# Ten issue edges on VectorE and ScalarE in a decoder step that TensorE fills

## The chip, the cores and the metric

The kernel runs on one core of a Trainium2 chip. Its engines are TensorE (PE in the profile; PEld is its weight load), VectorE (DVE), ScalarE (ACT), GpSimd (POOL), and SyncE (SP), whose queue issues nearly all DMAs. Each engine takes the instructions of its own queue in the order in which the program lists them; an instruction that waits for another engine holds up what stands behind it. The metric is the time of one execution on the device in microseconds (us), as the median of several runs. A profiled execution gives the trace; times of the trace count from the start of its span.

## The reference

The kernel computes one layer of a hybrid decoder for a prompt of 2048 tokens and for 8 sequences of one further token each, all in fp32, with a model width of 1024:

```
xn = rmsnorm(x, norm1_g);  z = xn @ w_in                 # 1024 -> 512 | 512 | 512 | 128 | 128
xr, gr, q, k, v = split(z)
xc = causal_conv4(xr);  r, i = sigmoid(block_diag(xc))   # real-gated LRU, a scan over the tokens
rec = lru(xc, r, i) * gelu(gr)
att = windowed_attention(q, k, v, sinks)                 # self + 128 previous tokens, 8 heads, 2 kv heads
mix = concat(rmsnorm(rec), rmsnorm(att));  h = x + mix @ w_out
hn = rmsnorm(h, norm2_g)
y = h + (silu(hn @ w_gate) * (hn @ w_up)) @ w_down       # d_ff 2816
return rmsnorm(y, final_norm_g), new k, v, conv and LRU states
```

## The kernel before

**Numbers as pairs.** Every operand of a large matmul is kept as two tiles, hi (a rounded copy) and lo (what the rounding left). mm3 at L398 makes one product out of three matmuls: hi by hi, hi by lo, lo by hi. So each operand passes through a copy on ScalarE that writes hi and a subtraction on VectorE or GpSimd that writes lo: split (L418) for the normed input xn, pth and ptl (L970, L971) for attention's transposed probabilities, hn (L565, L566) for the feed-forward input, fh and fl (L1365, L1366) for its middle, w_g and w_u (L1209, L1210) for its weights.

**Stages.** The tokens are cut into four stretches s = 0 to 3 of 520 or 512 tokens (the first holds the 8 single tokens too). For each stretch there is the input projection ("ip"), the convolution and the LRU (xc at L773, gates g, scans), the attention by blocks of 128 tokens and by kv head ("s" scores, "pt" transposes, "o" outputs; block 14 of kv head 1 has the tiles pth14_1_0 and ptl14_1_0), the norms of both groups (sums of squares by sq_ at L430, columns by L441 and L442, a broadcast "bc" by matmuls), and the output projection "op", which VectorE adds to the residual xres (L1072, for the last stretch L1119 and L1120). These stages run interleaved, up to about 690 us. Then the feed-forward takes three groups of tokens and eleven pairs of columns blocks; its first two factors are computed by Strassen's scheme (Winograd's form) with seven products each: sums of loaded blocks make the operands (m, s_g, s_u), products go to ps_g and ps_u, and their sums to c_g and c_u (L1395, L1416 to L1423), Silu (L1374) and the product of both (L1377) follow, and then the down projection "pd" and "pw".

**What sets the order.** Generators yield a time and what they wait for; that time becomes the priority of the instructions that follow, and a list scheduler with a timeline of its own then decides, engine by engine, which instruction comes next. `PE_ORDER`, a written list of all matmuls, is the exception: order_pe() ties each matmul behind the one listed before it. Such a tie is made by behind(later, earlier), a dependency without a semaphore: it fixes the order of the two in the schedule and makes no engine wait. VectorE, ScalarE, GpSimd and SyncE have no such list, and stand as the scheduler put them. "ones" matmuls in the list (w_...) only keep TensorE running.

Tiles come from small pools: two xs tiles and two sq tiles, three raw tiles, five weight pairs, one PSUM tile each for t, o and m, two for s, three for acc. A DMA that loads into a tile waits until the tile's last readers are done.

Of the kernel before, what the change touches and what calls it, by code (L numbers as in the profile page):

```python
# [7 lines left out]
F32 = mybir.dt.float32  # L8
F32R = mybir.dt.float32r
AF = mybir.ActivationFunctionType  # L10
# [15 lines left out]
EPS = 1e-6  # L26
# [255 lines left out]
def hybrid_step(tc, xT, xR, vecs, cst, gatew, win, wout, wgate, wup, wdown, kT, vC, ck, cv, sconv, sh0,  # L282
# [4 lines left out]
    with ExitStack() as ctx:  # L287
# [63 lines left out]
        def col(i):  # L351
            return vec[:, i:i + 1]
# [72 lines left out]
        def add_square(acc, v, T, first, name, eng=None, stage=sq_stage):  # L425
            if first:
                nc.scalar.square(acc[:, :T], v)
            else:
                sq = stage(f"sq_{name}")
                nc.scalar.square(sq[:, :T], v)  # L430
                return (eng or nc.gpsimd).tensor_tensor(acc[:, :T], acc[:, :T], sq[:, :T], op=ALU.add)

        def rstd_cols(acc, w, nt, which, out, name, lead=None, pin=False):
            ps = m_tile(f"st_{name}")
            with ahead(lead):
                for j in range(nt):
                    r = mm(f"st_{name}", ps[:w, j:j + 1], acc[:, j * w:(j + 1) * w], avg[:, which:which + 1],
                                         start=True, stop=True)
                    if pin and j == 0:
                        keep(r)  # L440
            nc.vector.tensor_scalar(out, ps[:w, :nt], EPS, None, ALU.add)  # L441
            nc.gpsimd.tensor_tensor(out, out, nhalf[:w, :nt], op=ALU.pow)  # L442

        def row_bcast(cols, w, nt, name, lead=None, keep_ps=False, pin=False):
# [16 lines left out]
        def eng(x):  # L461
            return nc.gpsimd if x == "P" else nc.vector
# [91 lines left out]
        def hn_load(gi, rs, place, t, dt, stage=None):  # L554
            nn = HALVES[gi][0][1]
            for i, r in enumerate(rs):
                for kk in range(4):
                    yield t + dt * (i + kk / 4), ("mixed", gi)
                    x = stage(f"m{gi}_{r}_{kk}")[:, :nn] if stage else None
                    hi, lo = next(place)[:, :nn], next(place)[:, :nn]  # L560
                    if not stage:
                        x = lo.bitcast(F32)
                    with ahead(F_LEAD[8]):
                        nc.sync.dma_start(x, mixed[gi, r - 1, :, kk, :nn])
                    nc.scalar.copy(hi, x)  # L565
                    (eng(E_HN[kk]) if gi else nc.vector).tensor_tensor(  # L566
                        lo, x, hi.bitcast(F32), op=ALU.subtract)
                    hn[gi, r, kk] = hi, lo
                fire(("hn", gi, r))
# [3 lines left out]
        with ExitStack() as actx:  # L573
# [128 lines left out]
            def prep(s):  # L702
                c0, T, nbl, w, nt = SUBS[s]
                t0, dt = T_IP[s] - L_PREP, D_PREP
                xn = state[s]["xn"] = []
                for k in range(KD):
                    yield t0 + dt * k
                    xs = xsp.tile([P, TM], F32, tag="xs", name=f"xs{s}_{k}")
                    with ahead(10):
                        d = nc.sync.dma_start(xs[:, :T], xT[:, k, c0:c0 + T])  # L710
                        if s == 1:
                            keep(d)
                    xt = bigp.tile([P, 2, TM], F32R, tag="big", name=f"xn{s}_{k}")
                    split(xt[:, 0, :T], xt[:, 1, :T], xs[:, :T], col(V_G1 + k))
                    xn.append(xt)
                fire(("xn", s))
                yield t0 + dt * KD, ("sums", s)
                norm_rows(s, None, state[s].pop("sums"))

            def row_sums(s):  # L720
                c0, _, _, w, _ = SUBS[s]
                sums = ap1.tile([P, 2, 4], F32, tag=f"xsums{s % 2}", name=f"xsums{s}")
                for k in range(KD):
                    yield T_RS[s - 1] + D_RS[s - 1] * k
                    xt = xsp.tile([P, TM], F32, tag="xs", name=f"xt{s}_{k}")[:, :512]
                    j, h = k // 2, k % 2
                    with ahead(L_RS):
                        nc.sync.dma_start(xt, xR[c0 + j * w:c0 + (j + 1) * w, h * 512:h * 512 + 512])
                    nc.scalar.activation(xt, xt, AF.Square, scale=1.0 / 32, accum_out=sums[:, h, j:j + 1])
                state[s]["sums"] = sums  # L730
                fire(("sums", s))

# [22 lines left out]
            def rec_chunk(s, c):  # L755
# [14 lines left out]
                    nc.scalar.activation(xc[:, 512:T], scv[:, c, 0, :], AF.Identity, bias=col(V_CB + c), scale=cw[0])  # L770
                for j in (1, 2, 3):
                    n = T if j == 3 else 512
                    nc.vector.scalar_tensor_tensor(xc[:, :n], xr[:, j:j + n], cw[j], xc[:, :n], ALU.mult, ALU.add)  # L773
# [144 lines left out]
            def attn_item(s, b, kv, t):  # L918
# [19 lines left out]
                for g2 in range(2):  # L938
                    ps = s_tile(f"s{gb}_{kv}_{g2}")
                    for gi in range(2):  # L940
                        g = g2 * 2 + gi
                        o = ps[:, gi * 256:gi * 256 + kn]
                        ks = slice(b * P + k0, b * P + k0 + kn)
                        with ahead():
                            mm(f"s{gb}_{kv}_{g2}", o, qst[:, g, :], KK[:, kv, ks], start=True, stop=False)
                            mm(f"s{gb}_{kv}_{g2}", o, qst[:, g, :], KL[:, kv, ks], start=False, stop=True)
                    for gi in range(2):
                        g = g2 * 2 + gi
                        nc.vector.tensor_tensor_reduce(  # L949
                            sc[:, g, :kn], ps[:, gi * 256:gi * 256 + kn], mask[:, k0:k0 + kn], -SCALE, ns[:, g:g + 1],  # L950
                            ALU.add, ALU.min, accum_out=mx[:, 0, g:g + 1])
                if last:
# [9 lines left out]
                for i, kb in enumerate(kbs):  # L962
                    yield t + D_ATT[2] + i
                    pt = t_tile(f"pt{gb}_{kv}_{kb}")
                    with ahead():
                        for g in range(G):
                            tr(f"pt{gb}_{kv}_{kb}", pt[:, g * P:(g + 1) * P], sc[:, g, i * P:(i + 1) * P], ident)
                    ph = ap4.tile([P, 512], F32R, tag="pth", name=f"pth{gb}_{kv}_{kb}")
                    pl = ap4.tile([P, 512], F32R, tag="ptl", name=f"ptl{gb}_{kv}_{kb}")
                    nc.scalar.copy(ph, pt)  # L970
                    nc.vector.tensor_tensor(pl, pt, ph.bitcast(F32), ALU.subtract)  # L971
# [11 lines left out]
                nc.vector.tensor_tensor(ov, pov[hr], ov, ALU.add)  # L983
                fire(("o", s, b, kv))

            def decode(t):
# [70 lines left out]
            def out_unit(s, m):  # L1057
# [8 lines left out]
                for n0, nn in nbl:  # L1066
# [2 lines left out]
                        mm3(f"op{s}_{m}_{n0}", ps[:, :nn], wt, k, mix[k][:, 0, n0:n0 + nn], mix[k][:, 1, n0:n0 + nn],  # L1069
                            k == 0, k == KD - 1)  # L1070
                    with ahead(L_EV):
                        nc.vector.tensor_tensor(xs[:, n0:n0 + nn], xs[:, n0:n0 + nn], ps[:, :nn], ALU.add)  # L1072
# [12 lines left out]
            def out_half(s, m, i):  # L1085
# [31 lines left out]
                yield t + 1, ("at", s, "bc")  # L1117
                with ahead(L_EV):
                    nc.vector.tensor_tensor(ps[:, :T], ps[:, :T], state[s]["late"][:, :T], ALU.mult)  # L1119
                    nc.vector.tensor_tensor(xs[:, :T], xs[:, :T], ps[:, :T], ALU.add)  # L1120
                nc.scalar.dma_start(hs[:, m, c0:c0 + T], xs[:, :T])

            def fin_a():
# [39 lines left out]
        with ExitStack() as bctx:  # L1163
# [181 lines left out]
            def products(gi, p, x):  # L1345
# [24 lines left out]
                def finished(h, n, src=None):  # L1370
                    v = C[h, n][:, :nn]
                    src = v if src is None else src
                    if not up:
                        nc.scalar.activation(v, src, AF.Silu)  # L1374
                        return
                    g = gss[gi, p][h, n][:, :nn]
                    (nc.vector if p == NPAIR - 1 or src is not v else eng(E_MUL[2 * h + n])).tensor_tensor(  # L1377
# [20 lines left out]
                for i, r in enumerate(PRODS):  # L1398
# [15 lines left out]
                    with ahead(F_LEAD[5]):  # L1414
# [3 lines left out]
                            add(c11, c21, ps)  # L1418
                            finished(0, 0)
                        elif r == 6:  # L1420
                            nc.scalar.copy(c12, ps)  # L1421
# [292 lines left out]
```

## Time and profile before

| | |
|---|---|
| median of 3 runs | 2063.5 us (2061.77 to 2065.69) |
| the profiled execution | 2061.57 us, its span 2059.8 us |
| busy: PE / DVE / ACT / POOL | 98% / 71% / 46% / 44% of the span |
| mean granted clock of TensorE | 0.997 of full speed |
| moved by DMA | 450.98 MB, mean 219 GB/s |

The span is that of the trace; the profiled execution's time has a little more around it. A row of the timeline gives the start, the duration, the engine, the line of the kernel, the operation, out<-in with the tiles' names, and in brackets how long the engine had been idle before the row and what released it. Neighbouring instructions of one kind are drawn together (x4). Rows overlap a little on an engine since the next instruction begins while the last one's writes end, so that two rows' starts are often closer than the first one's duration.

### The profile page before, as it was taken

What the parts mean: (1) busy time and instruction counts of PE and PEld (TensorE: products, weight loads), DVE (VectorE), ACT (ScalarE), POOL (GpSimd) and SP (SyncE); (2) the same over time, 40 slices, a digit from 0 to 9 for tenths busy, and PEclk for the clock granted to TensorE, in tenths of its full rate; (3) what the DMA queues carried; (4) which work ended last, traced back from release to release, by engine and by line L of the source; (5) the groups of instructions that cost most, each with busy time, mean ns of one, the idle gap of its engine ahead of it and who ended that gap; (6) DMA issues with size and microseconds to landing.
All of it is one profiled execution on the core that took longest, in us unless ns stands there. A gap on an engine that the chain in (4) does not pass through costs nothing.

```text
span 2059.8 us, 34860 instructions
## 1 busy us (share of the span) xinstructions
PE 2018.7 (98%) x12319; PEld 1909.6 (93%) x12319; DVE 1463.0 (71%) x2694; ACT 944.2 (46%) x1960; POOL 905.3 (44%) x799
## 2 busy tenths in 40 slices
PE   9999999999999999999999999999999999999998
PEld 9988787878777899999999999999999999999998
DVE  6877986767985766666654667778768666777675
ACT  6774774563563543344334533334335433433343
POOL 4311342020131786667656645556456522322333
PEclk9999999999999999999999999999999999999999
DMA  9864584576687856566546677676677675566652
GB/s 320 288 222 144 189 273 160 180 234 204 217 262 266 312 198 212 206 216 203 206 174 211 233 257 246 231 232 221 222 251 264 212 250 195 182 194 196 198 179 96
DMA packets 208991, 450.98 MB, mean 219 GB/s; under 512 B 25232, under 2 KB 82720, under 8 KB 208800
## 3 DMA queue, kind: packets, MB, share of 16 engines
q1 hardware_dynamic: 205184, 445.73, 64.8%
q10 hardware_dynamic: 3632, 3.02, 0.4%
q8 instruction: 97, 1.59, 0.3%
q14 instruction: 78, 0.64, 0.1%
HBM read 335.89 MB, written 113.84 MB: 218 GB/s over the span
## 4 chain that ended last, share of the span: by engine, by line
PE 73%; DVE 12%; DMA 7%; ACT 4%; issue 3%; POOL 2%; SPq 0%; DVEq 0%; ACTq 0%; POOLq 0%
PE ps_u L390 18%; PE ps_g L390 18%; PE pw L390 10%; PE ip L390 10%; PE pd L390 9%; PE op L390 3%; DMA n<-hs 3%; DMA mixed<-n 1%; DMA xs<-in_xT 1%; DVE sc L949 1%; PE o L390 1%; DVE n L509 1%; PE pt L395 1%; DVE xn L420 1%; DVE sc L960 1%
## 5 line engine op out<-in xcount | busy, mean ns | idle before, releaser
L390 PE MATMUL ps_g<-hn,w_g 128*128 128x342 f32 (+1 forms) x2772 | 489.5, 320 | 4.9 <-DVE c_g L1395 1.3
L390 PE MATMUL ps_u<-hn,w_u 128*128 128x342 f32 (+1 forms) x2772 | 479.7, 319 | 1.3 <-ACT c_u L1421 0.8
L390 PEld LDWEIGHTS ps_g<-hn,w_g 128*128 128x128 f32 x2772 | 445.0, 188 | 6.9 <-DVE c_u L1395 1.8
L390 PEld LDWEIGHTS ps_u<-hn,w_u 128*128 128x128 f32 x2772 | 444.0, 188 | 2.0 <-ACT c_u L1421 1.0
L390 PE MATMUL ip<-xn,w_in 128*128 128x512 f32 (+1 forms) x1680 | 354.9, 359 | 1.7 <-ACT xn L419 1.5
L390 PEld LDWEIGHTS ip<-xn,w_in 128*128 128x128 f32 x1680 | 271.5, 191 | 45.8 <-issue 3.8
L1485 DVE TENSOR_TENSOR y<-y,pw 128x342 f32<-128x342 f32 x504 | 238.8, 504 | 73.5 <-PE pw L390 72.8
L390 PE MATMUL pd<-fh,w_d 128*128 128x344 f32 (+1 forms) x960 | 239.6, 320 | 1.7 <-DVE y L1454 1.6
L390 PE MATMUL op<-mix,w_out 128*128 128x512 f32 (+1 forms) x960 | 203.4, 357 | 0.8 <-DVE rrec L750 0.7
L390 PEld LDWEIGHTS op<-mix,w_out 128*128 128x128 f32 x960 | 155.3, 188 | 29.8 <-issue 5.2
L390 PEld LDWEIGHTS pd<-fh,w_d 128*128 128x128 f32 x960 | 168.3, 188 | 2.8 <-DVE y L1454 2.5
L1454 DVE TENSOR_TENSOR y<-y,pd 128x344 f32<-128x344 f32 (+1 forms) x240 | 117.6, 507 | 73.5 <-PE pd L390 65.9
L390 PE MATMUL pw<-fh,wd 128*128 128x342 f32 x576 | 165.7, 320 | 2.0 <-DVE y L1485 2.0
L390 PE MATMUL pd<-fl,w_d 128*128 128x344 f32 (+1 forms) x480 | 153.4, 320 | 0.0
L1366 DVE TENSOR_TENSOR fl<-c_u,fh 128x342 fp32r<-128x342 f32 (+1 forms) x132 | 109.0, 830 | 48.9 <-ACT fh L1365 48.8
L1210 POOL TENSOR_TENSOR w_u<-ru,w_u 128x512 fp32r<-128x512 f32 x44 | 59.2, 1346 | 182.6 <-ACT w_u L1209 139.6
L1377 POOL TENSOR_TENSOR c_u<-c_u,c_g 128x342 f32<-128x342 f32 (+1 forms) x60 | 60.4, 1006 | 173.6 <-DVE c_u L1395 137.9
L1365 ACT CAST fh<-c_u 128x342 fp32r<-128x342 f32 (+1 forms) x132 | 62.9, 480 | 158.4 <-POOL c_u L1377 63.8
L390 PE MATMUL pw<-t,wd 128*128 128x342 f32 x648 | 126.8, 320 | 3.0 <-DVE t L1366 2.3
L1395 DVE TENSOR_TENSOR c_u<-c_u,ps_u 128x342 f32<-128x342 f32 (+1 forms) x99 | 50.3, 508 | 99.9 <-PE ps_u L390 98.5
L390 PEld LDWEIGHTS pw<-t,wd 128*128 128x128 f32 x648 | 106.0, 188 | 5.0 <-DVE t L1366 3.4
L390 PEld LDWEIGHTS pw<-fh,wd 128*128 128x128 f32 x576 | 105.4, 189 | 2.7 <-DVE y L1485 2.6
(316 smaller groups left out, 3507.4 us busy)
## 6 DMA issues: line engine op xcount, KB each, us to landing
w_g<-split_g SPq DMA_DIRECT2D x88, 512.0 KB, 4.3
w_u<-split_u SPq DMA_DIRECT2D x88, 512.0 KB, 4.9
w_in<-split_w SPq DMA_DIRECT2D x84, 512.0 KB, 3.4
rg<-in_wgate SPq DMA_DIRECT2D x110, 256.0 KB, 3.0
ru<-in_wup SPq DMA_DIRECT2D x110, 256.0 KB, 3.2
w_out<-split_w SPq DMA_DIRECT2D x48, 512.0 KB, 4.7
split_g<-w_g SPq DMA_DIRECT2D x44, 512.0 KB, 3.4
split_u<-w_u SPq DMA_DIRECT2D x44, 512.0 KB, 2.7
```

The lines of the kernel that those rows point to most:

```text
L390: r = nc.tensor.matmul(*args, **kw)
L395: r = nc.tensor.transpose(*args)
L420: return r, nc.vector.scalar_tensor_tensor(lo, src, g, hi.bitcast(F32), ALU.mult, ALU.subtract)
L509: nc.vector.scalar_tensor_tensor(x, x, col(V_G2 + k), bc[n][:, :nn], ALU.mult, ALU.mult)
L949: nc.vector.tensor_tensor_reduce(sc[:, g, :kn], ps[:, gi * 256:gi * 256 + kn], mask[:, k0:k0 + kn], -SCALE, ns[:, g:g + 1], ALU.add, ALU.m ...
L1210: lo_eng.tensor_tensor(w[:, 1, :], src, w[:, 0, :].bitcast(F32), op=ALU.subtract)
L1365: nc.scalar.copy(hi, v)
L1366: nc.vector.tensor_tensor(lo, v, hi.bitcast(F32), ALU.subtract)
L1377: (nc.vector if p == NPAIR - 1 or src is not v else eng(E_MUL[2 * h + n])).tensor_tensor(v, src, g, op=ALU.mult)
L1395: nc.vector.tensor_tensor(o, a, b, op)
L1454: r = nc.vector.tensor_tensor(ys[gi, n, m], ys[gi, n, m], ps, ALU.add)
L1485: nc.vector.tensor_tensor(v, v, ps, ALU.add)
```

## The change

A list of ten pairs is added. Each is (later, earlier): `behind` ties the first behind the second in the schedule. The names are written down where the instructions are made, in a dictionary `seen`. No instruction is added or taken out, TensorE's list is the same, and the ten edges have no semaphores. Each pair lies on one engine: sq_, xt, pth and act and c are ScalarE's, the others VectorE's.

```diff
+AFTER = [
+    ("xl2_5", "xc1_2_3"), ("xt3_1", "pth5_1_1"),
+    ("sm6_1_0", "ptl5_1_1"), ("xa2_7_0", "eps_rc3"),
+    ("sq_h2_3", "pth14_0_1"), ("sq_rc3_2", "pth14_1_0"),
+    ("act0_0_00", "cg0_0_6"), ("xl2_7", "ptl5_1_0"),
+    ("sm1_1_1", "ov0_0"), ("hl0_7_3", "xb3_7"),
+]
...
+        seen = {}
+
+        def order_engines():
+            for later, earlier in AFTER:
+                behind(seen[later], seen[earlier])
...
-                nc.scalar.square(sq[:, :T], v)
+                seen[f"sq_{name}"] = nc.scalar.square(sq[:, :T], v)
...
-            nc.vector.tensor_scalar(out, ps[:w, :nt], EPS, None, ALU.add)
+            seen[f"eps_{name}"] = nc.vector.tensor_scalar(out, ps[:w, :nt], EPS, None, ALU.add)
...
-                        nc.scalar.activation(v, src, AF.Silu)
+                        seen[f"act{gi}_{p}_{h}{n}"] = nc.scalar.activation(v, src, AF.Silu)
...
             order_pe()
+            order_engines()
```

The other names are written down in the same way: xl (the lo part of xn, L420), xt (squares for the row sums, L729), xc (the convolution, L773), sm (scores, L949), pth and ptl (L970, L971), ov (the attention output, L983), xa and xb (the residual adds, L1072 and L1120), hl (the lo part of hn, L566), and c..._6 (the copy at L1421).

With the edges the scheduler decides anew around each of them, also on queues that have no edge. The rows differ between about 85 and 130 us, 245 and 300, 598 and 632, and 674 and 732 us of the trace; elsewhere the order is as before. Three places follow. A name ends in a running number of the tile; behind it stands the tile's shape. (The line numbers of the kernel with the change are higher by 7 to 16.)

VectorE near 620 us, before: xres2_7 is the last residual tile of stretch 2, rccols3 the columns for the norm of stretch 3's recurrent group, rrec that group.

```order
L971 TENSOR_TENSOR ptl14_1_1_6748<-pt14_1_1_6742,pth14_1_1_6747 128x512
L958 RECIPROCAL mx15_1_6818<-mx15_1_6818 128x4
L960 TENSOR_SCALAR sc15_1_6817<-sc15_1_6817,mx15_1_6818 128x256 x4
L1072 TENSOR_TENSOR xres2_7_6263<-xres2_7_6263,op2_7_0_6412 128x512
L441 TENSOR_SCALAR rccols3_6272<-st_rc3_6273 128x4
L983 TENSOR_TENSOR ratt_145<-o14_1_6751,ratt_145 64x4x128
L971 TENSOR_TENSOR ptl15_0_0_6795<-pt15_0_0_6787,pth15_0_0_6794 128x512
L852 SCALAR_TENSOR_TENSOR rrec_144<-rrec_144,vec_99,rb_rc3_6280 128x512 x4
```

The same place with the change:

```order
L975 TENSOR_SCALAR sc15_1_6817<-sc15_1_6817,mx15_1_6818 128x256 x4
L454 TENSOR_SCALAR rccols3_6272<-st_rc3_6273 128x4
L1087 TENSOR_TENSOR xres2_7_6263<-xres2_7_6263,op2_7_0_6412 128x512
L998 TENSOR_TENSOR ratt_145<-o14_1_6751,ratt_145 64x4x128
L986 TENSOR_TENSOR ptl15_0_0_6795<-pt15_0_0_6787,pth15_0_0_6794 128x512
L867 SCALAR_TENSOR_TENSOR rrec_144<-rrec_144,vec_99,rb_rc3_6280 128x512 x4
```

rccols3 has moved in front of xres2_7.

ScalarE near 700 us, before: hn0_1_10 is a feed-forward operand, fh0_0_00 the hi part of the first column block's middle, made from c_u0_0_00.

```order
L565 CAST hn0_1_9_7762<-m0_4_2_7766 128x344
L565 CAST hn0_1_10_7771<-m0_4_3_7770 128x344
L1209 CAST w_g0_1_6_8055<-s2_g0_1_8037 128x512
L1209 CAST w_g0_1_5_8061<-s1_g0_1_8035 128x512
L1421 COPY c_u0_0_01_7171<-ps_u0_0_1_7951 128x344
L1374 ACTIVATE c_g0_0_10_7160<-ps_g0_0_1_7813 128x344
L1209 CAST w_g0_1_1_8002<-rg0_1_00_7878 128x512
L1576 ACTIVATE hacc3_8272<-h3_0_8273 128x512
L1365 CAST fh0_0_00_7162<-c_u0_0_00_7170 128x344
```

The same place with the change:

```order
L578 CAST hn0_1_9_7762<-m0_4_2_7766 128x344
L1225 CAST w_g0_1_6_8055<-s2_g0_1_8037 128x512
L1225 CAST w_g0_1_5_8061<-s1_g0_1_8035 128x512
L1437 COPY c_u0_0_01_7171<-ps_u0_0_1_7951 128x344
L1381 CAST fh0_0_00_7162<-c_u0_0_00_7170 128x344
L578 CAST hn0_1_10_7771<-m0_4_3_7770 128x344
L1592 ACTIVATE hacc3_8272<-h3_0_8273 128x512
L1594 ACTIVATE h3_1_8311<-h3_1_8311 128x512
L1390 ACTIVATE c_g0_0_10_7160<-ps_g0_0_1_7813 128x344
```

hn0_1_10 has moved behind fh0_0_00. On VectorE its lo part has moved in the same way behind c_u0_0_00 and fl0_0_00. TensorE's list has these rows there, before and with the change alike:

```order
L390 MATMUL ps_u0_0_2_7968<-hn0_0_5_6402,w_u0_0_2_7861 128x344
L390 MATMUL ps_u0_0_2_7968<-hn0_0_4_6397,w_u0_0_2_7861 128x344
L390 MATMUL ps_g0_0_1_7813<-hn0_1_9_7762,w_g0_0_4_7827 128x344 x2
L390 MATMUL ps_g0_0_1_7813<-hn0_1_10_7771,w_g0_0_4_7827 128x344 x3
L390 MATMUL ps_u0_0_5_8021<-hn0_1_0_7693,w_u0_0_5_7908 128x344 x4
```

The three with hn0_1_10 follow right behind the last of ps_u0_0_2, from which c_u0_0_00 is made.

More of the change, by code (lines that the diff above doesn't have):

```diff
@@ L565, in hn_load @@
                     nc.scalar.copy(hi, x)
-                    (eng(E_HN[kk]) if gi else nc.vector).tensor_tensor(
+                    seen[f"hl{gi}_{r}_{kk}"] = (eng(E_HN[kk]) if gi else nc.vector).tensor_tensor(
                         lo, x, hi.bitcast(F32), op=ALU.subtract)
@@ L713, in prep @@
                     xt = bigp.tile([P, 2, TM], F32R, tag="big", name=f"xn{s}_{k}")
[L714 removed]
+                    _, seen[f"xl{s}_{k}"] = split(xt[:, 0, :T], xt[:, 1, :T], xs[:, :T], col(V_G1 + k))
                     xn.append(xt)
@@ L969, in attn_item @@
                     pl = ap4.tile([P, 512], F32R, tag="ptl", name=f"ptl{gb}_{kv}_{kb}")
-                    nc.scalar.copy(ph, pt)
-                    nc.vector.tensor_tensor(pl, pt, ph.bitcast(F32), ALU.subtract)
+                    seen[f"pth{gb}_{kv}_{kb}"] = nc.scalar.copy(ph, pt)
+                    seen[f"ptl{gb}_{kv}_{kb}"] = nc.vector.tensor_tensor(pl, pt, ph.bitcast(F32), ALU.subtract)
                     pts.append((kb, ph, pl))
@@ L982, in attn_item @@
                 nc.scalar.copy(ov, pov[lr])
-                nc.vector.tensor_tensor(ov, pov[hr], ov, ALU.add)
+                seen[f"ov{gb}_{kv}"] = nc.vector.tensor_tensor(ov, pov[hr], ov, ALU.add)
                 fire(("o", s, b, kv))
@@ L1071, in out_unit @@
                     with ahead(L_EV):
-                        nc.vector.tensor_tensor(xs[:, n0:n0 + nn], xs[:, n0:n0 + nn], ps[:, :nn], ALU.add)
+                        seen[f"xa{s}_{m}_{n0}"] = nc.vector.tensor_tensor(xs[:, n0:n0 + nn], xs[:, n0:n0 + nn],
+                                                                          ps[:, :nn], ALU.add)
                 yield t + 5.5, ("hq", s, m - 1)
@@ L1420, in products @@
                         elif r == 6:
-                            nc.scalar.copy(c12, ps)
+                            seen[f"c{name}_6"] = nc.scalar.copy(c12, ps)
                         elif r == 5:
```

10 lines of the change are left out of this document (6 added, 4 removed).

## The prediction

> **What bounds the kernel now.** I read the page first, for the engine that fills the span, and then the timeline of TensorE (PE) for the places where it does not.
>
> ```profile
> span 2059.8 us, 34860 instructions
> ...
> PE 2018.7 (98%) x12319; PEld 1909.6 (93%) x12319; DVE 1463.0 (71%) x2694; ACT 944.2 (46%) x1960; POOL 905.3 (44%) x799
> ...
> PE 73%; DVE 12%; DMA 7%; ACT 4%; issue 3%; POOL 2%; SPq 0%; DVEq 0%; ACTq 0%; POOLq 0%
> ```
>
> TensorE is busy for 98% of the span and makes up most of the chain that ended last. 41 us of it are idle, so that is all that a better order on the other engines could win. The change adds no instruction, takes none away, and leaves TensorE's own order as it is: its price can only be TensorE waits that go, move or come, and the clock at which it runs behind them. These are the rows of TensorE's timeline at the ten places that the edges concern (start, duration, operation; in brackets the idle time before it and what ended it):
>
> ```profile
> 85.87 0.50 PE L390 MATMUL o<-pth,vt 128*128 128x512 f32 x1 [0.74 <-DVE ratt L983]
> ...
> 254.96 1.12 PE L390 MATMUL g<-xc,gw 128*128 128x512 f32 x2 [1.27 <-DVE xc L773]
> 268.41 0.63 PE L395 MATMUL pt<-cs,sc 128*128 128x128 f32 x4 [1.14 <-DVE ptl L971]
> 275.55 0.50 PE L390 MATMUL o<-ptl,vt 128*128 128x512 f32 x1 [0.97 <-DVE ptl L971]
> ...
> 601.92 0.50 PE L390 MATMUL o<-pth,vt 128*128 128x512 f32 x1 [0.35 <-ACT pth L970]
> ...
> 612.94 0.50 PE L390 MATMUL o<-pth,vt 128*128 128x512 f32 x1 [1.14 <-ACT pth L970]
> ...
> 622.63 0.39 PE L390 MATMUL bc_rc<-ones 128*128 128x256 f32 x1 [1.16 <-DVE rccols L441]
> 623.73 2.08 PE L390 MATMUL bc_rc<-cs,rccols 128*128 128x128 f32 x8 [0.71 <-POOL rccols L442]
> ...
> 685.36 4.04 PE L390 MATMUL ps_g<-hn,w_g 128*128 128x344 f32 x24 [1.18 <-DVE xres L1120]
> ...
> 693.06 4.04 PE L390 MATMUL ps_g<-hn,w_g 128*128 128x344 f32 x24 [0.93 <-ACT c_g L1421]
> ```
>
> Together they are 0.74+1.27+1.14+0.97+0.35+1.14+1.16+0.71+1.18+0.93 = 9.6 us, 0.47% of the time. Two more views decide how much of that can be kept. The stretches (columns: length; busy time of PE, PEld, DVE, ACT, POOL; PE's clock; DMA share; GB/s):
>
> ```profile
> 240.00:276.00 36.00, 32.06 (x231) 28.78 (x230) 33.79 (x60) 31.45 (x62) 19.07 (x16) 1.00 0.87 295
> ...
> 683.00:706.00 23.00, 18.00 (x109) 16.57 (x108) 17.40 (x23) 12.19 (x25) 13.68 (x11) 1.00 0.96 340
> ```
>
> and the granted clock of TensorE in stretches of 2 us (PE busy, clock, DMA share, GB/s), which between the first microseconds and the tail leaves 1.00 in two places only:
>
> ```profile
> 22.00:24.00 2.00, 2.00 (x13) 0.65 0.88 340
> 24.00:26.00 2.00, 2.00 (x11) 0.50 0.95 318
> ...
> 622.00:624.00 2.00, 0.66 (x2) 0.84 1.02 407
> 624.00:626.00 2.00, 2.00 (x9) 0.50 0.98 387
> 626.00:628.00 2.00, 2.00 (x15) 0.81 0.05 18
> ```
>
> Each drop costs 2 x (1 - clock), summed: 0.70+1.00 = 1.7 us, and 0.32+1.00+0.38 = 1.7 us. The second follows the waits of 1.16 and 0.71 us at 622 to 624, about 1.9 us idle within some 3 us.
>
> **The change part by part.**
>
> *Scores behind the output add (sm1_1_1, at 85).* One score instruction leaves the queue in front of ptl0_1_1 and ov0_0, for which the wait of 0.74 stands. Its price:
>
> ```profile
> 272.54 0.47 DVE L949 CUSTOM_DVE_ANT_0 sc<-s,cs,nsk 128x256 f32<-128x256 f32 x1
> ...
> 112.27 0.63 ACT L729 ACTIVATE xt<-xt 128x512 f32<-128x512 f32 x1
> 112.80 0.19 ACT L729 ACTIVATION_READ_ACCUMULATOR xt<-xt 128x1 f32 x1
> ```
>
> That gains about 0.4 us. But behind it the scheduler sets the squares xt2_5 and xt2_7 on ScalarE in front of the gate activation that has to free the PSUM tile of a gate matmul near 117, and the squares wait for loads: up to two of them, 2 x 0.82 = 1.6 us. Bounds -0.4 and +1.6; I take +0.3, since a stall there begins from a place that has little slack but not none.
>
> *xl2_5, xt3_1, xl2_7, sm6_1_0 (247 to 276).* In 240:276 VectorE is busy 33.8 of 36 us. Reordering takes no work off it, so a shorter wait at 254.96 comes back at 268.41, where the same queue is late. Gained is only what is moved behind the last operand of the stretch, ptl5_1_1: two score instructions of 0.41 (row above, without the overlap), 0.8 us. Bounds 0 (the next VectorE row is late by as much) and -3.4 (1.27+1.14+0.97); I take -0.8.
>
> *sq_h2_3, sq_rc3_2, xres2_7 behind rccols3 (598 to 629).* The rows:
>
> ```profile
> 611.65 0.63 ACT L430 ACTIVATE sq_rc<-rrec 128x512 f32<-128x512 f32 x1
> ...
> 621.81 0.69 DVE L1072 TENSOR_TENSOR xres<-xres,op 128x512 f32<-128x512 f32 x1 [1.88 <-DMA xres<-in_xT]
> 622.42 0.15 DVE L441 TENSOR_SCALAR rccols<-st_rc 128x4 f32<-128x4 f32 x1
> ...
> 626.46 2.08 DVE L852 SCALAR_TENSOR_TENSOR rrec<-rrec,vec,rb_rc 128x512 f32<-128x512 f32 x3 [1.18 <-ACT rb_rc L458]
> ...
> 622.65 1.02 POOL L442 TENSOR_TENSOR rccols<-rccols,nhalf 128x4 f32<-128x4 f32 x1 [5.11 <-DVE rccols L441]
> ```
>
> Two squares of 0.63 leave the queue in front of the casts pth14_0_1 and pth14_1_0: the waits of 0.35 and 1.14 go. rccols3 stood behind xres2_7, which waited 1.88 us for its load; ahead of it, it runs as soon as its matmuls end, and with the pow of 1.02 the broadcast can start about 2 us earlier. What is late next is VectorE again: the load still lands near 621.8, then come xres2_7, ratt and ptl15_0_0 at 0.6 each, and rrec can start near 623.6 in place of 626.46, a gain of 2.8. Bounds -3.4 (0.35+1.14+1.16+0.71, the waits entire) and -1.0 (only the two squares); I take -2.5, nearest to the load's row. The squares that moved delay the load of a later xres by less than its slack.
>
> *hl0_7_3 and act0_0_00 (680 to 705).* The rows:
>
> ```profile
> 680.79 1.60 DVE L566 TENSOR_TENSOR hn<-m,hn 128x344 fp32r<-128x344 f32 x1
> ...
> 684.11 0.51 DVE L566 TENSOR_TENSOR hn<-m,hn 128x344 fp32r<-128x344 f32 x1
> 684.53 0.68 DVE L1120 TENSOR_TENSOR xres<-xres,op 128x512 f32<-128x512 f32 x1
> ...
> 689.40 0.50 DVE L1395 TENSOR_TENSOR c_g<-c_g,ps_g 128x344 f32<-128x344 f32 x1
> ...
> 696.07 1.78 DVE L1210 TENSOR_TENSOR w_g<-rg,w_g 128x512 fp32r<-128x512 f32 x1
> ...
> 690.51 1.28 ACT L1374 ACT_TABLE_LOAD   x1
> ...
> 689.96 2.17 PE L390 MATMUL ps_u<-hn,w_u 128*128 128x344 f32 x12 [0.56 <-DVE c_g L1395]
> ```
>
> The hn subtraction of up to 1.60 now stands behind xres3_6, so the wait of 1.18 at 685.36 goes. But VectorE has no gap from 680.79 to 689.90, and the same set of instructions still stands in front of c_g at 689.40: the matmul at 689.96 waits as long as before, its 0.56 becoming about 1.7. The copy c_g0_0_01 now runs ahead of the table load of 1.28, so the wait of 0.93 at 693.06 goes too; but the last hn0_1_7 part now stands behind the w_g subtraction of 1.78, and its matmuls, due near 695, wait for it. Net at the end of ps_u0_0_2: bounds -1.0 and +1.2, I take +0.2. The bounds lie apart because an hn subtraction takes 0.51 or 1.60 by what runs beside it on GpSimd.
>
> *A new wait behind it (705).* The order shown with the change has hn0_1_10 behind fh0_0_00 on ScalarE and behind fl0_0_00 on VectorE; TensorE's order is fixed, and ps_g0_0_1 with hn0_1_10 stands right behind ps_u0_0_2. Both fh and fl need c_u0_0_00, which needs ps_u0_0_2:
>
> ```profile
> 705.11 0.95 PE L390 MATMUL ps_g<-hn,w_g 128*128 128x344 f32 x5
> ...
> 705.31 0.51 DVE L1395 TENSOR_TENSOR c_u<-c_u,ps_u 128x344 f32<-128x344 f32 x1 [1.68 <-PE ps_u L390]
> ...
> 705.90 1.36 POOL L1377 TENSOR_TENSOR c_u<-c_u,c_g 128x344 f32<-128x344 f32 x1 [1.12 <-DMA rd<-in_wdown]
> ...
> 707.90 0.48 ACT L1365 CAST fh<-c_u 128x344 fp32r<-128x344 f32 x1
> ```
>
> So before the three hn0_1_10 matmuls (the last of the row at 705.11, from 705.43) there now run the add 0.5, from 705.90 the multiply 1.36 to 707.26, the cast fh 0.48 and the cast of hn0_1_10 of the same size to 708.2, and its subtraction of 0.51 to 708.7: 708.7 - 705.5 = 3.2 us of new wait. Bounds 2.7 (the first matmul needs the cast alone) and 4.3 (the subtraction takes 1.60). I take +3.2.
>
> *The clock behind it.* The longest wait in the rows above is 1.27 us, and about 1.9 us idle in two waits dropped the clock at 623. One wait of 3.2 us is more than both, so I take the whole price of a drop, +1.7, with bounds 0 and 1.7. The Trainium skill, in "TensorE: Matmul & The Clock Gate", Part 1, ties the half clock to at least one idle window of about 3.4 us, free-running; by the letter of that rule a wait of 3.2 us broken by a matmul would not drop it, and this sum would be 1.7 lower. The rows at 622 to 628 speak against reading it so strictly.
>
> *Sum.* +0.3 -0.8 -2.5 +0.2 +3.2 +1.7 = +2.1 us. The profiled execution took 2061.57 us (span 2059.8 and 1.8 around it), so it would be 2063.7; the median of the three runs, 2063.5, lies 1.9 above it, so the median would be **2065.6**. Behind 706 the order is the same as before, and TensorE runs with few waits, so the sum should reach the end.
>
> **The rivals.**
>
> *The waits go and stay away (faster).* If VectorE's contention with GpSimd eases where the order changed, all 9.6 us could go. For it speaks that each edge takes the instruction out that stood in front of the late one; against it, the full VectorE in 240:276 and the gapless stretch before 689. With the new wait and its clock the time would be 2063.5 - 9.6 + 4.9 = 2058.8; it decides for faster once the waits keep off more than 9.0 us, and if hn0_1_10 came in time as well it would be 2053.9.
>
> *The gain at 622 does not reach the feed-forward (slower).* In 683:706 the DMA engines are 96% busy at 340 GB/s. If the loads of hn's sources land no earlier than now, the 2.5 us end there as a wait for them, and the new wait comes on top: +2.1 + 2.5 = 4.6; with the subtraction at 1.60, 1.1 more, 5.7: 2068 to 2069. It decides when the cast of hn0_1_5, which waits for its load now, runs at its old time.
>
> *No drop of the clock.* Everything else as forecast: +0.4, 2063.9. This is the rule of the Trainium skill named above, taken as a mechanism here: the wait at 705 is cut in two by one matmul.
>
> *The contention.* A wait of 4.3 in place of 3.2 is inside the second rival. The Trainium skill, in "SBUF — State Buffer", Who interferes with whom, says that a VectorE instruction with two SBUF inputs is blocked by a GpSimd one that reads SBUF; the 0.51 and 1.60 of the same hn subtraction agree.
>
> **How the numbers follow.** Forecast 0.34, gain that stays 0.20, gain that is swallowed 0.30, no drop 0.16. A change within 0.2% (4.1 us), from 2059.4 to 2067.6, is about what this kernel's runs cannot tell from none. Faster by more than that is the first rival: 0.20. Slower by more is the second, 0.30, and the upper part of the forecast (the new wait at 4.3), 0.06: 0.36. The rest, 0.44, is the same. The range leaves out the far half of the first rival and the far tail of the second: 2057.0 to 2071.0. The likeliest case alone reaches from 2063 to 2068.
>
> **What would show it.** In the profile after: no wait on L441 near 622 and rrec near 623; xres3_6 ahead of an hn row near 683 and c_g at nearly its old distance behind it; then TensorE idle for about 3 us in front of ps_g, released by ScalarE's or VectorE's hn, near 705, and a clock of 0.5 for 3 us behind it. The prediction is wrong if that idle time is not there, if the 2.5 us are not kept until 683, or if the stretch 240:276 gives back its 3.4.

## The result and the profile after

With the ten edges the median is 2070.56 us (2069.29 to 2073.81, 7 runs); the kernel before had 2063.37 in as many runs beside it. The ratio is 1.0037, with a 95% interval from 1.0027 to 1.0048: 7 to 8 us slower. (A ratio is given with its own interval and is not the quotient of the two medians; the two differ by up to some 0.1%, in e9 and e10 below. Small differences are read from the ratios.) The profiled execution of the changed kernel took 2071.99 us, and before 2061.57: one lies 1.4 us above its median and the other 1.8 below, so that the two traces differ by some 3 us more than the medians do.

The page of the kernel after: span, busy time, and the chain that ended last.

```profile
span 2070.2 us, 34846 instructions
...
PE 2023.7 (98%) x12319; PEld 1915.3 (93%) x12319; DVE 1462.8 (71%) x2694; ACT 945.1 (46%) x1960; POOL 906.8 (44%) x799
...
PE 77%; DVE 9%; DMA 7%; ACT 3%; issue 2%; POOL 2%; SPq 0%; DVEq 0%; ACTq 0%; POOLq 0%
```

The other engines' busy times are those of before; the span is 10.4 us longer, and of these 5.0 us are TensorE's own busy time: the same matmuls, at a lower clock in some places. (The 14 instructions fewer are semaphore instructions of the other engines.) TensorE's timeline after shows waits where there were none:

```profile
117.68 0.70 PE L397 MATMUL g<-xc,gw 128*128 128x260 f32 x2 [0.91 <-ACT ia L803]
...
275.28 0.68 PE L397 MATMUL o<-pth,vt 128*128 128x512 f32 x1 [2.53 <-ACT pth L985]
...
626.79 1.16 PE L397 MATMUL bc_rc<-cs,rccols 128*128 128x128 f32 x8 [0.71 <-POOL rccols L455]
...
693.64 2.16 PE L397 MATMUL ps_u<-hn,w_u 128*128 128x344 f32 x12 [2.95 <-DVE c_g L1411]
...
700.89 0.91 PE L397 MATMUL ps_g<-hn,w_g 128*128 128x344 f32 x3 [1.64 <-DVE hn L579]
704.32 1.22 PE L397 MATMUL ps_u<-ones 128*128 128x256 f32 x4 [2.52 <-DVE c_g L1411]
...
714.76 0.42 PE L397 MATMUL ps_g<-hn,w_g 128*128 128x344 f32 x1 [2.60 <-ACT hn L578]
715.36 0.63 PE L397 MATMUL ps_g<-hn,w_g 128*128 128x344 f32 x2 [0.18 <-DVE hn L579]
```

Since TensorE's list of matmuls is the same, each matmul of the one trace has its fellow in the other, and the difference of their starts tells how late TensorE is at each place:

| place (time before) | late by, in front | behind | what happened |
|---|---|---|---|
| 86 to 118 us | +0.2 | +0.75 | 0.4 gained at 86, a wait of 0.91 at 117 |
| 213 to 219 | +0.8 | +2.0 | TensorE's clock at half behind a wait that both kernels have |
| 247 to 276 | +2.0 | +3.65 | three waits shorter, one of 2.53 new, and half clock behind it |
| 276 to 600 | +3.65 | +4.4 | absorbed near 425, late again near 560 to 600 |
| 600 to 630 | +4.4 | +2.7 | the wait for rccols3 and the half clock behind it are gone |
| 685 to 705 | +2.7 | +6.5 | 2.95, 1.64 and 2.52 of waits in place of 1.18, 0.56, 0.93, 1.32 and 1.01, and half clock |
| 705 | +6.5 | +9.8 | the wait for hn0_1_10 |
| 706 to 719 | +9.8 | +11.3 | half clock again |
| 719 to the end | +11.3 | +10.4 | slightly absorbed |

The clock rows (length, PE busy, clock, DMA share, GB/s) that belong to it:

```profile
704.00:706.00 2.00, 1.68 (x7) 0.50 0.73 181
706.00:708.00 2.00, 2.00 (x9) 0.50 1.02 396
708.00:710.00 2.00, 2.00 (x12) 0.77 0.88 263
...
714.00:716.00 2.00, 1.06 (x4) 0.94 0.99 393
716.00:718.00 2.00, 2.00 (x8) 0.50 0.27 109
718.00:720.00 2.00, 2.00 (x11) 0.71 0.41 128
```

The wait for hn0_1_10 runs as the order says. The timelines of VectorE, GpSimd and ScalarE at that place, after:

```profile
711.89 0.51 DVE L1411 TENSOR_TENSOR c_u<-c_u,ps_u 128x344 f32<-128x344 f32 x1 [5.29 <-PE ps_u L397]
...
712.48 1.34 POOL L1393 TENSOR_TENSOR c_u<-c_u,c_g 128x344 f32<-128x344 f32 x1 [4.75 <-DVE c_u L1411]
...
713.85 0.48 ACT L1381 CAST fh<-c_u 128x344 fp32r<-128x344 f32 x1 [0.66 <-POOL c_u L1393]
714.24 0.47 ACT L578 CAST hn<-m 128x344 fp32r<-128x344 f32 x1
...
714.79 0.51 DVE L579 TENSOR_TENSOR hn<-m,hn 128x344 fp32r<-128x344 f32 x1
```

The sum at 711.89, the product at 712.48, fh at 713.85, and only then the cast and the subtraction of hn0_1_10, for which TensorE waits 2.60 and 0.18 us.

### The profile page after: what moved, and what is told of

The parts are those of the page before. It is cut to its first block, busy times and chain, and to the rows that moved or that the text cites. A ratio compares the mean times of both kernels' runs of the same rounds, so it can differ in the third digit from the quotient of the medians.

```text
span 2070.2 us, 34846 instructions
## 1 busy us (share of the span) xinstructions
PE 2023.7 (98%) x12319; PEld 1915.3 (93%) x12319; DVE 1462.8 (71%) x2694; ACT 945.1 (46%) x1960; POOL 906.8 (44%) x799
## 3 DMA queue, kind: packets, MB, share of 16 engines
q10 hardware_dynamic: 3632, 3.02, 0.4%
## 4 chain that ended last, share of the span: by engine, by line
PE 77%; DVE 9%; DMA 7%; ACT 3%; issue 2%; POOL 2%; SPq 0%; DVEq 0%; ACTq 0%; POOLq 0%
PE ps_u L397 19%; PE ps_g L397 18%; PE pw L397 10%; PE pd L397 10%; PE ip L397 9%; PE op L397 5%; DMA n<-hs 3%; DMA mixed<-n 1%; PE o L397 1%; PE s L397 1%; PE pt L402 1%; DVE n L522 1%; PE g L397 1%; DVE hn L579 1%; DMA xt<-in_xR 1%
```

## The experiments

The ten edges fall into groups whose effects on the queues don't overlap: each group alone moves the same rows as it does among the ten. So the groups can be tried one by one. The seventh edge, on the copy, was run only together with others. All are written against the kernel before (the AFTER list is empty there), and each ratio is to the kernel before, run beside it.

**Which group costs the time.** First the ten without the one edge at the start of the feed-forward, and this edge alone.

```diff
 AFTER = [
     ...
-    ("sm1_1_1", "ov0_0"), ("hl0_7_3", "xb3_7"),
+    ("sm1_1_1", "ov0_0"),
 ]
```

> The changed kernel with nine edges, all but hl0_7_3 behind xb3_7; hn0_1_10 then stands ahead of fh0_0_00 again, as before, and the queues between 650 and 730 us are those of before but for the copy c_g0_0_01. Theory A, that this edge makes the loss (the reordered start of the feed-forward, the wait for hn0_1_10 and the half clock behind it, +8.7 us between 628 and 719 us in the two traces): the median falls by 7 to 9 us to about 2062.5, no better than 1 us below the kernel before. Theory B, that the loss is made upstream, around 212 to 276 us, and the feed-forward only shows it: it stays at 2067 to 2070.

Measured: 2061.89 us, ratio 0.9998 (0.9988 to 1.0009).

```diff
+AFTER = [("hl0_7_3", "xb3_7")]
```

> The kernel before with the one edge hl0_7_3 behind xb3_7. Theory A: 7 to 9 us slower than before, 2070 to 2072, with TensorE idle for about 3 us in front of the hn0_1_10 matmuls and its clock at 0.5 behind. Theory B: within 3 us of before, 2062 to 2066.

Measured: 2069.86 us, ratio 1.0031 (1.0019 to 1.0043). Theory A holds in both directions: without this edge the loss is gone, and alone it makes some six sevenths of it (0.31 of 0.37%). Theory B falls. Edge seven, the copy c_g0_0_01, is among those that stay in e1, so it does no harm that can be seen.

The three edges of the norm, and those of the attention:

```diff
+AFTER = [
+    ("xa2_7_0", "eps_rc3"), ("sq_h2_3", "pth14_0_1"), ("sq_rc3_2", "pth14_1_0"),
+]
```

> The kernel before with the three edges at 598 to 629 us (xres2_7 behind rccols3, sq_h2_3, sq_rc3_2). The prediction: the 2.5 us of this stage are gained and kept, 2060.9. The trace after (4.4 us late at 604, 2.6 late at 627): 1.8 gained, 2061.6. Rival: a gain here is taken back by the start of the feed-forward, 2063.4.

Measured: 2059.56 us, ratio 0.9989 (0.9979 to 0.9999): a gain of about 2.3 us, as forecast for this stage, and kept to the end.

```diff
+AFTER = [
+    ("xl2_5", "xc1_2_3"), ("xt3_1", "pth5_1_1"),
+    ("sm6_1_0", "ptl5_1_1"), ("xl2_7", "ptl5_1_0"),
+]
```

> The kernel before with the four edges at 247 to 276 us (xl2_5, xt3_1, sm6_1_0, xl2_7). The prediction: 0.8 gained, 2062.6. The trace after: a new wait of 2.5 us in front of o5_1<-pth5_1_1, because that cast now stands behind xt3_2, which waits for its load, and a half clock behind the wait; 1 to 3 us lost, of which 1 may be absorbed later: 2064 to 2066.

Measured: 2063.91 us, ratio 1.0009 (0.9998 to 1.0019): about 1.9 us lost, with an interval that just reaches no change. In its trace the wait of 2.53 us stands in front of the same matmul as after. The traces agree: between 246 and 320 us TensorE falls behind the trace before by 0.6 to 3.3 us in the nine traces that have these four edges (1.5 in the mean), and by -0.8 to +0.7 in the six others.

Of the norm's three edges the one on rccols3 alone, and the edge of the scores:

```diff
+AFTER = [("xa2_7_0", "eps_rc3")]
```

> The kernel before with the one edge xres2_7 behind rccols3. If rccols3's place is the larger part of e3's gain of 3.0 us: 1.5 to 2.5 gained, 2060 to 2061, with no wait on rccols3 near 622. Rival, that the two squares of e3 make the gain (1.14 and 0.35 of waits): 2062 to 2062.6.

Measured: 2059.51 us, ratio 0.9986 (0.9975 to 0.9998). This edge makes the gain; the two squares add nothing that shows. The traces tell where it comes from. Between 600 and 650 us the clock falls in eight of the nine traces without this edge, for 3.4 or 6.8 us, and in none of the seven with it: not only the wait for rccols3 is gained, but the half clock behind it too.

```diff
+AFTER = [("sm1_1_1", "ov0_0")]
```

> The kernel before with the one edge sm1_1_1 behind ov0_0. The prediction: +0.3 (between -0.4 and +1.6). The trace after: 0.4 gained at 86 us, a wait of 0.9 to 1.3 in front of a gate matmul at 117: +0.5 to +0.9 at 118, 2063 to 2063.5 if nothing absorbs it.

Measured: 2063.5 us, ratio 1.0004 (0.9990 to 1.0017), not told from no change. Its trace has the wait at 117 (1.22 us). The four groups add to +0.31 +0.09 -0.11 +0.04 = +0.33%, and the ten together measured +0.37%.

**What the edge at the feed-forward costs by its parts.** It was given two more edges that put hn0_1_10 back where it stood, and nothing else:

```diff
+AFTER = [
+    ("hl0_7_3", "xb3_7"), ("adu0_0", "hl0_4_3"), ("wh_g0_1_6", "hh0_4_3"),
+]
...
-                nc.scalar.copy(w[:, 0, :], src)
+                seen[f"wh_{name}"] = nc.scalar.copy(w[:, 0, :], src)
...
-                    nc.scalar.copy(hi, x)
+                    seen[f"hh{gi}_{r}_{kk}"] = nc.scalar.copy(hi, x)
...
-                            add(c11, c21, ps)
+                            seen[f"ad{name}"] = add(c11, c21, ps)
```

> Run e2 (the edge hl0_7_3 alone, 2069.9) with two more edges that put hn0_1_10 back ahead: its cast ahead of the w_g0_1_6 cast on ScalarE, its subtraction ahead of the c_u0_0_00 sum on VectorE; the rest of the queues is that of e2. Theory A1, that the wait for hn0_1_10 and the second half clock behind it are the larger part: the wait in front of ps_g0_0_1<-hn0_1_10 is gone, 4 to 5 us come back, 2065 to 2066, and what is left over 2062.5 is the reordering before it (waits at ps_u0_0_1, hn0_1_7, c_g0_0_01). Rival, that the order before 705 is all of it: 2068 to 2070. Rival, that the wait is all of it: 2062 to 2063.

Measured: 2064.81 us, ratio 1.0014 (1.0005 to 1.0024). Beside e2 that is 5.1 us less by the medians and 3.5 by the ratios. TensorE's timeline of this run:

```profile
702.03 1.22 PE L395 MATMUL ps_u<-ones 128*128 128x256 f32 x4 [2.52 <-DVE c_g L1409]
...
709.93 0.94 PE L395 MATMUL ps_g<-hn,w_g 128*128 128x344 f32 x5
```

The last five ps_g matmuls, with hn0_1_9 and hn0_1_10, run without a wait, and the clock does not fall behind them. So the wait and the clock behind it are the larger part of the loss, as far as the two intervals, which overlap a little, can tell; the wait of 2.52 us in front of the ones, which comes earlier, is still there, and so are 1.4 thousandths of the time.

In the second run TensorE was kept busy while it waits:

```diff
+AFTER = [("hl0_7_3", "xb3_7")]
...
-g0_0_3:12 g0_0_4 w_ps_u0_0_2:4 g0_0_4:5 u0_0_2:9 g0_0_4 u0_0_2 u0_0_6:12 u0_0_2:2 g0_0_4:5 u0_0_5:12 u0_0_7:12
+g0_0_3:12 g0_0_4 w_ps_u0_0_2:4 g0_0_4:5 u0_0_2:9 g0_0_4 u0_0_2 u0_0_6:12 u0_0_2:2 g0_0_4:2 w_ps_u0_0_5:20 g0_0_4:3 u0_0_5:12 u0_0_7:12
```

> Run e2 with twenty matmuls on ones (128x256, into the PSUM tile of ps_u0_0_5 before its own matmuls) put into TensorE's order in front of the three hn0_1_10 matmuls: TensorE is busy while it waits there, nothing else changes its place. If the half clock behind the wait costs what its rows say (1.5 to 1.7 us), the clock stays at 1.00 behind 716 and the time falls to about 2068.3. Rival, that the clock behind the wait costs nothing since other engines are late there too: 2070.

Measured: 2067.20 us, ratio 1.0024 (1.0014 to 1.0033): 2.7 us less than e2 by the medians, 1.4 by the ratios, with intervals that overlap. Its timeline and clock there:

```profile
707.63 2.65 PE L393 MATMUL ps_u<-ones 128*128 128x256 f32 x20 [0.30 <-DVE c_u L1407]
710.12 1.02 PE L393 MATMUL ps_g<-hn,w_g 128*128 128x344 f32 x3
```

```profile
708.00:710.00 2.00, 2.00 (x20) 1.00 0.47 193
710.00:712.00 2.00, 1.88 (x13) 1.00 0.85 334
712.00:714.00 2.00, 2.00 (x15) 1.00 0.02 6
```

The clock stays at 1.00 behind the filled gap, where e2 and the kernel after fall to 0.50. The 1.4 to 2.7 us, with matmuls that compute nothing, fit the 1.7 of the clock rows, but since the intervals overlap the time alone does not show them.

**Why the attention's edges lose.** In e4's timeline ScalarE has, in front of the cast for which TensorE waits:

```profile
271.09 0.81 ACT L781 ACTIVATE xc<-xr,vec 128x512 f32<-128x512 f32 x1 [1.59 <-DVE ix L805]
271.81 0.61 ACT L741 ACTIVATE xt<-xt 128x512 f32<-128x512 f32 x1
...
272.42 0.56 ACT L984 CAST pth<-pt 128x512 fp32r<-128x512 f32 x1
```

The edge took xt3_1 out of the cast's way, but xc1_3 and xt3_2 still stand in front of it. xc1_3 waits because the scheduler has turned round two instructions of VectorE, ix1_2, which reads the tile that xc1_3 writes, and q21_1. First before, with xc1_3 on ScalarE, then in e4:

```profile
268.52 0.68 DVE L791 SCALAR_TENSOR_TENSOR ix<-ia,xc 128x512 f32<-128x512 f32 x1
269.12 1.78 DVE L801 SCALAR_TENSOR_TENSOR q<-q,ra 128x512 f32<-128x512 f32 x1
...
269.34 0.80 ACT L768 ACTIVATE xc<-xr,vec 128x512 f32<-128x512 f32 x1
```

```profile
267.91 1.44 DVE L815 SCALAR_TENSOR_TENSOR q<-q,ra 128x512 f32<-128x512 f32 x1
269.28 1.77 DVE L805 SCALAR_TENSOR_TENSOR ix<-ia,xc 128x512 f32<-128x512 f32 x1
```

I first took xt3_2, of which I believed that it waited for its load (the rows show no wait of its own behind xc1_3):

```diff
 AFTER = [
     ("xl2_5", "xc1_2_3"), ("xt3_1", "pth5_1_1"),
     ("sm6_1_0", "ptl5_1_1"), ("xl2_7", "ptl5_1_0"),
+    ("xt3_2", "pth5_1_1"),
 ]
```

> Run e4 (the four edges at 247 to 276 us, 2063.9) with one more, xt3_2 behind pth5_1_1, which takes the square that waits for its load out of the queue in front of that cast. If that square is what made the wait of 2.5 us in front of o5_1<-pth5_1_1: the wait is gone, the stage ends 1 to 2 us ahead of before, and the time is 2061 to 2062.5. Rival, that the cast is late for another reason (xc1_3 in front of it, or VectorE): 2063.9.

Measured: 2064.43 us, ratio 1.0010 (0.9998 to 1.0022). No gain, and a wait of 1.92 us is left: shorter by 0.61 us, the time of that square itself. ScalarE there:

```profile
271.17 0.81 ACT L782 ACTIVATE xc<-xr,vec 128x512 f32<-128x512 f32 x1 [1.59 <-DVE ix L806]
271.89 0.56 ACT L985 CAST pth<-pt 128x512 fp32r<-128x512 f32 x1
```

My reason fell. xc1_3 waits as long for ix1_2. So the next run took xc1_3 away instead:

```diff
 AFTER = [
     ("xl2_5", "xc1_2_3"), ("xt3_1", "pth5_1_1"),
     ("sm6_1_0", "ptl5_1_1"), ("xl2_7", "ptl5_1_0"),
+    ("xi1_3", "pth5_1_1"),
 ]
...
-                nc.scalar.activation(xc[:, :512], xr[:, 0:512], AF.Identity, bias=col(V_CB + c), scale=cw[0])
+                seen[f"xi{s}_{c}"] = nc.scalar.activation(xc[:, :512], xr[:, 0:512], AF.Identity, bias=col(V_CB + c), scale=cw[0])
```

> Run e4 (the four edges at 247 to 276 us) with one more on ScalarE: the first convolution product of xc1_3 behind the cast pth5_1_1. Run e7 showed that cast behind xc1_3, and xc1_3 idle 1.59 us until VectorE's ix1_2 was done, which now stands behind q21_1. If that is the cause of the wait in front of o5_1<-pth5_1_1 (1.9 us in e7, 2.5 in e4): the wait is gone, TensorE is 1 to 2 us ahead of before at 276 us, and the time falls from 2064 to about 2061.5. Rival, that VectorE, full there, gives the lateness back at the next operand: 2063 to 2064.

Measured: 2063.84 us, ratio 0.9995 (0.9986 to 1.0005): the same as before, and again a wait of 1.91 us, now behind the other one:

```profile
270.54 0.63 ACT L742 ACTIVATE xt<-xt 128x512 f32<-128x512 f32 x1 [1.68 <-DMA xt<-in_xR]
...
271.16 0.57 ACT L985 CAST pth<-pt 128x512 fp32r<-128x512 f32 x1
```

Both are late by the same amount, for different reasons. So both were put behind the cast:

```diff
+    ("xi1_3", "pth5_1_1"), ("xt3_2", "pth5_1_1"),
```

> Run e4 (the four edges at 247 to 276 us) with both edges of e7 and e9: xt3_2 and the first product of xc1_3 behind the cast pth5_1_1. In e7 the cast stood behind xc1_3, idle 1.59 us for VectorE's ix1_2; in e9 behind xt3_2, idle 1.68 us for its load: each alone was enough for 1.9 us of wait. If these two together make the wait: it is gone from in front of o5_1<-pth5_1_1, TensorE is 1.5 to 2 us ahead of before at 276, and the time is 2 us under e4, a ratio to before of 0.999. Rival, that the next operand (ptl5_1_1 on VectorE) is as late: a wait of 1 to 2 us in front of o5_1<-ptl5_1_1, ratio 1.000 or above.

Measured: 2065.11 us, ratio 1.0008 (1.0000 to 1.0017). The wait in front of o5_1 is gone, and between 255 and 276 us TensorE wins 1.4 us on the trace before (from 1.7 late to 0.2 late). But the time did not fall, and the expected place of the rival was also wrong: the lateness comes back one block later. TensorE and ScalarE of this run:

```profile
284.86 0.50 PE L398 MATMUL o<-pth,vt 128*128 128x512 f32 x1 [1.63 <-ACT pth L986]
```

```profile
283.00 0.63 ACT L743 ACTIVATE xt<-xt 128x512 f32<-128x512 f32 x1 [3.02 <-DMA xt<-in_xR]
...
284.24 0.57 ACT L986 CAST pth<-pt 128x512 fp32r<-128x512 f32 x1
```

The squares that wait for loads now stand in front of the next cast, pth6_0_0, 3.02 us for a load. As the rows read, the loads of xt3 set the pace of ScalarE's queue here, and an edge only chooses the cast that pays. That was not tried: no run issued the loads earlier, or gave ix1_2 its old place.

**What of it can be had.** Eight edges (without hl0_7_3 and sm1_1_1) with the mending of e7, e9 and e13 in turn:

```diff
 AFTER = [
     ("xl2_5", "xc1_2_3"), ("xt3_1", "pth5_1_1"),
     ("sm6_1_0", "ptl5_1_1"), ("xl2_7", "ptl5_1_0"),
     ("xa2_7_0", "eps_rc3"), ("sq_h2_3", "pth14_0_1"),
     ("sq_rc3_2", "pth14_1_0"), ("act0_0_00", "cg0_0_6"),
+    ("xt3_2", "pth5_1_1"),
 ]
```

> Eight of the ten edges (all but hl0_7_3 and sm1_1_1) and xt3_2 behind pth5_1_1. If the parts add up: e3's gain of 2 to 3 us and e7's of up to 1.5: 2058 to 2060, faster than both kernels. Rival, that a gain at 276 is swallowed by the full VectorE and the loads of 545 to 600 us: that of e3 alone, 2059.6 to 2061.

Measured: 2061.35 us, ratio 0.9998 (0.9987 to 1.0008).

> Eight of the ten edges (all but hl0_7_3 and sm1_1_1) and the edge of run e9. If the parts add: e3's 3.0 us and what e9 gains, 2058 to 2059.5, faster than both kernels and than e3. Rival, that a gain at 276 does not pass the stretch 545 to 600 us: as e3, 2059.5 to 2061.

Measured, with ("xi1_3", "pth5_1_1") in place of ("xt3_2", "pth5_1_1"): 2062.03 us, ratio 0.9986 (0.9974 to 0.9998).

> Eight of the ten edges (all but hl0_7_3 and sm1_1_1) with both edges of e13. If the gains of e3 and e13 add: a ratio of 0.9975 to 0.998. Rival, that the stretch up to 600 us swallows what is gained at 276: that of e3 and e11 alone, 0.9985 to 0.999.

Measured, with both: 2062.99 us, ratio 1.0001 (0.9990 to 1.0012). None is better than the norm's edges alone; no form of the attention's four edges shows a gain. e10 has the ratio of e11, but by the medians, beside the same runs of the kernel before, it is 2.5 us behind it. The best versions are e3 and e11, 0.9989 and 0.9986, which beat the kernel before by about 2 to 3 us and, by the ratios, the changed one by some 10. For the one edge on rccols3 this is a small change with a clear mechanism; its interval ends at 0.9998.

## Why the prediction was right and wrong

It forecast +2.1 us, no change that can be told, and gave 0.36 to a slower kernel; it is +7.2 us by the medians. 2070.56 lies within the range, near its end, but the likeliest case was not the one that came. That the range holds it is luck: its upper end and most of the 0.36 stood for the second rival, the norm's gain lost before the feed-forward, and that did not happen. By the ratios of the runs of single groups the scores came out at +0.8 us (taken +0.3), the attention +1.9 (taken -0.8), the norm -2.3 (taken -2.5), and the start of the feed-forward +6.4 (e2; taken +0.2 +3.2 +1.7 = +5.1). The interval of e4 leaves out what was taken; that of e2, 3.9 to 8.9 us, does not, so that for this stage the trace has to decide. By its own terms, with the lateness of the table:

- *Scores (taken +0.3, bounds -0.4 and +1.6).* About +0.5 in the trace, by the wait that it named at 117 us (ia, behind a square).
- *247 to 276 us (taken -0.8, bounds 0 and -3.4).* **Failed**: +1.7 in the trace and +0.09% alone (e4). The step that failed is "Gained is only what is moved behind the last operand of the stretch". It looked at VectorE alone, and there the waits did shrink (1.27 to 0.31 and 0.23, 1.14 to 0.70, 0.97 to nothing). On ScalarE the cast pth5_1_1 was left behind xc1_3, which now waited 1.58 us, and behind xt3_2, whose load is as late (1.68 us in e9); e7, e9 and e13 show this. The new wait of 2.53 us takes back all that the others give, and the half clock behind it, in five of the nine traces with these edges, comes on top. Its upper bound, 0, left no loss at all; its reason, that the next VectorE row would be as late, named neither ScalarE nor the clock.
- *598 to 629 us (taken -2.5, bounds -3.4 and -1.0).* Right in size: -1.7 in the trace, -2.3 alone (e3), and VectorE's sequence is that of the prediction. After: rccols3 first, then xres2_7 on its load, then rrec.

```profile
625.49 0.15 DVE L454 TENSOR_SCALAR rccols<-st_rc 128x4 f32<-128x4 f32 x1
626.54 0.69 DVE L1087 TENSOR_TENSOR xres<-xres,op 128x512 f32<-128x512 f32 x1 [0.90 <-DMA xres<-in_xT]
...
628.61 3.31 DVE L867 SCALAR_TENSOR_TENSOR rrec<-rrec,vec,rb_rc 128x512 f32<-128x512 f32 x4
```

But the squares gave nothing: in front of the casts' matmuls two waits of 0.52 and 0.53 us are left, and e11 has the gain without them. And no term held the half clock at 623, 1.7 us in its own rows, which went too. So the size is right in part by luck. The second rival fell: the gain reached the end.
- *680 to 705 us (taken +0.2, bounds -1.0 and +1.2).* **Failed in its size**: +3.8. The mechanism was right: the wait at 685 goes, and comes back in front of ps_u0_0_1, behind c_g on VectorE. But it was priced as if the same instructions took the same time. After, the three hn subtractions stand together beside GpSimd's sums, and two more stand in front of the c_g for which the ones wait:

```profile
686.24 4.09 DVE L579 TENSOR_TENSOR hn<-m,hn 128x344 fp32r<-128x344 f32 x3
...
701.18 2.66 DVE L579 TENSOR_TENSOR hn<-m,hn 128x344 fp32r<-128x344 f32 x2
703.76 0.50 DVE L1411 TENSOR_TENSOR c_g<-c_g,ps_g 128x344 f32<-128x344 f32 x1
```

Before, TensorE had at this place:

```profile
698.41 0.40 PE L390 MATMUL ps_g<-hn,w_g 128*128 128x344 f32 x1 [1.32 <-DVE c_g L1395]
699.82 0.74 PE L390 MATMUL ps_u<-ones 128*128 128x256 f32 x4 [1.01 <-DVE c_g L1395]
```

The three took 4.09 us, where before they took 1.60, 0.51 and 1.01 in their places; so the wait in front of ps_u0_0_1 became 2.95 and not 1.7. The wait of 1.01 in front of the ones became 2.52, which no term held. Together the waits grew by 2.1 us. The rest, some 1.7 us, is half clock ahead of 705, which the prediction had only behind it. This part is not shown to be the edge's work: nine of the eleven runs without hl0_7_3 have a half clock there too (e3 below), and the trace before is one of the few without. That the hn subtractions are slow because of GpSimd is read from the rows and was not tried by itself. The Trainium skill's "SBUF — State Buffer", Who interferes with whom, has a VectorE instruction with two SBUF inputs contend with a GpSimd one that reads SBUF; the rows agree.
- *The new wait at 705 (taken +3.2, bounds 2.7 and 4.3).* Right: 3.3 in the trace.
- *The clock behind it (taken +1.7).* Right: 1.5 in the trace, and it is there in e2 and absent in e5 and e6. The rival by the letter of the clock rule in the Trainium skill ("TensorE: Matmul & The Clock Gate", Part 1: a whole idle window of some 3.4 us) fell: a wait of 2.60 us was enough.

So what made the kernel slower was seen from the order alone, at the right place and size; what was missed is that two stages in front of it, taken for a small gain and for even, lost some 2 us each, the second another 1.7 by a half clock that may be chance.

## What to carry to other kernels

An issue edge takes one instruction out of the way of a late operand, but the scheduler fills the place and moves what hangs on it: read, for each edge, everything that stands in front of the operand on its own queue afterwards, and for each of these what it waits for; with two blockers, taking one away shows little (e7, e9). An edge that holds back an operand can cost more than the wait that it removes, as hl0_7_3 did, when the held-back queue meets a matmul that is fixed by another list. Try edges one by one: of ten, one gained, one lost about twice as much, and the rest, run in groups, could not be told from nothing.

## What the runs showed of the hardware

A wait on TensorE is often paid twice. Behind two or three microseconds of idle time, in one wait or in several close together, the clock fell to 0.50 in many of these traces. By the clock rows it stayed there for 3.4 us (kernel before behind 623 us, 1.7 us lost), for 6.8 us (kernel after behind 702), or for 10.2 us (e13 behind 211: 5.1 us lost). In e6, where matmuls on ones fill the gap at 708, it stayed at 1.00.

But idle time alone doesn't decide. The rows of two runs at the same place of the program: e1 (all edges but hl0_7_3) was busy for 1.00 of 4 us, and its clock stayed:

```profile
698.00:700.00 2.00, 0.39 (x3) 1.00 1.05 414
700.00:702.00 2.00, 0.61 (x2) 1.00 1.04 404
702.00:704.00 2.00, 2.00 (x15) 1.00 0.98 354
```

e3 (the norm's edges) was busy for 1.67 of 4 us, and its clock fell:

```profile
694.00:696.00 2.00, 0.69 (x5) 1.00 1.09 388
696.00:698.00 2.00, 0.98 (x7) 1.00 0.93 369
698.00:700.00 2.00, 2.00 (x9) 0.51 0.99 295
```

At 213 to 219 us not even the program differs. e2's only edge acts behind 680 us, and up to there its order is that of the kernel before. The same thirteen matmuls stand behind the same waits of 0.78 and 1.73 us, first before, with the clock at 1.00, then in e2, where it fell to 0.50:

```profile
212.73 1.82 PE L390 MATMUL st_at<-ones 128*128 128x256 f32 x13 [1.73 <-ACT ia L788]
```

```profile
211.16 2.80 PE L393 MATMUL st_at<-ones 128*128 128x256 f32 x13 [1.73 <-ACT ia L799]
```

Six of the sixteen traces have a half clock there, and it bears no relation to the edges. So the same stall costs or does not cost 1.5 us and more from one execution to the next, and two profiles can differ by that without any cause in the program. The Trainium skill ("TensorE: Matmul & The Clock Gate", Part 1) has the window of the gate run free of the program, which agrees with these rows. It is one reason why single traces misled here by more than the effects that were looked for, and why the verdicts stand on ratios of several runs.
